# A hybrid Fourier/Hyena block on one core: the long convolution's first transform stage as two 64-row matmuls, and PSUM handed out in pairs of banks

## The chip, the cores and the metric

The kernel runs on 1 core of one Trainium2 chip. The metric is the device time in microseconds (us), the median over several executions. Everything is float32 at the borders; inside, some products use a split of each operand into two halves (`fp32r`), others are plain float32.

## What is computed

One layer of an encoder block over 2048 positions and 1024 channels. Cut to what matters here:

```
p   = rmsnorm(x) @ W_in               -> Fourier group | x1 | x2 | v   (512 columns each)
y_f = rmsnorm(Re(FFT2 of the Fourier group))
z   = v
for n, gate in enumerate((x1, x2)):   # 512 channels
    z = gate * (irfft(rfft(z, 4096) * rfft(k_n)) [:2048] + z * d_n)
y_h = rmsnorm(z)
x   = x + concat(y_f, y_h) @ W_out
x   = x + relu(rmsnorm(x) @ W_fc1)^2 @ W_fc2
out = rmsnorm(x)
```

The change sits in the loop over `n`, the two long convolutions. Each real transform of length 4096 is done as two small DFTs. The first one is a product with a table of 32 input rows, the same for every residue of the position; then comes a rearrangement, and then a second product with one 128x128 table for each of 32 frequencies.

## The kernel before, in words

The program is one Python function that writes out every instruction. A tile framework adds the semaphores and allots buffers; each engine then executes its own instructions strictly in the order in which they were written, save where the program raises the priority of a few lines (none of these are in the part that changes). The stages in order, with the time at which they lie in the profiled run:

- 0 to 413 us: two passes of `project` (lines 319 to 440), 32 + 32 accumulations `pu` of 24 matmuls each, and beside the first of them the filters' hidden layers and a product of weights.
- 413 to 618 us: `fourier` (449) and `filters` (499), which makes the spectra of the eight filters and stores them in DRAM.
- 618 to about 826 us: `hyena` (677), the convolutions.
- from there to the end at 2296 us: `project_out` (901), `fc1` (1116) and `fc2` (1233), long rows of 512-column matmuls.

**The convolutions.** `hyena` works through eight blocks, for n = 0, 1 and four groups of 128 channels (`ct`). The data lies in `zz`, 128 partitions by 16 by 512; a partition holds one of two halves of the positions (`sp`), one of 32 positions and one of two interleaved parts. A block has these steps:

- `first(c)`, lines 712 to 719, for c = 0 to 7: the first DFT for 16 channels. Two matmuls (line 718), one for each half `sp`, with the weights `e1[:, sp, :]` (128x128) and 256 moving columns each, into the left and right half of one PSUM bank `pz1`. The table `e1z` (lines 60 to 65) holds zeros in the 64 rows that belong to the other half, so half of each product is a sum of zeros. Then VectorE turns the bank into `G` (`turned`, lines 444 to 446, a stream transpose of 512 elements per partition).
- `second(q)`, lines 721 to 734, for q = 0 to 7: four matmuls of 128 columns (725) read `G`; ScalarE copies the result into `zs` with its halves exchanged (728, 729), VectorE multiplies it by the spectrum `ks` into `y` (731), GpSimd multiplies `zs` by `ks` (732), and one of the two adds both (733). `ks` is loaded by SyncE's DMA queue (704), with four buffers.
- `inverse(q)`, 736 to 742: four matmuls (741) read `y`; ScalarE copies into `V` (742).
- `turn(c)`, 744 to 747, for c = 0 to 7: VectorE turns `V` into `W`.
- `gate(q)`, 749 to 757, for q = 0 to 3: two matmuls of 64 output rows and 512 columns (754) into the upper and the lower half of the partitions of one bank `pb`; VectorE multiplies by the gate into `zz` (755).

The order is written out by hand (759 to 803). In round i, block i does `second(0)` to `second(7)`. Beside it run the `inverse` of the same block, three steps later (`LAG`), the `turn`s of block i-1, the four `gate`s of block i-2 at q = 1, and the `first`s of block i+1 as `FIRSTS` says: before, two at each of q = 0 and 1, one at each of q = 2, 3, 4 and 5. Block 0 does its eight `first`s ahead of round 0 (768, 769). `first` puts work on TensorE and VectorE alone; it issues no DMA.

**PSUM.** The memory that matmuls write has eight banks of 512 float32 per partition. Every stage takes its banks through one function (168, 169), a ring of eight tiles with one tag:

```
    def pa(nm):
        return ps.tile([P, 512], F32, tag="a", name=nm, bufs=8)
```

A tile's bank comes free when its last reader is done, and a matmul that opens a new tile waits for a free bank; what stands behind it on TensorE waits too. In the profile the names lose their numbers: `pz1` and `pz2` are both `pz`, `pk`, `pk1` and `pk2` are `pk`.

Of the kernel before, what the change touches and what calls it, by code (L numbers as in the profile page):

```python
# [10 lines left out]
F32 = mybir.dt.float32  # L11
# [118 lines left out]
P = 128  # L130
# [6 lines left out]
def hybrid_block(ctx: ExitStack, tc: tile.TileContext, A, out):  # L137
    nc = tc.nc
# [23 lines left out]
    ps = ctx.enter_context(tc.tile_pool(name="ps", bufs=2, space=PSUM))  # L162
    small = ctx.enter_context(tc.tile_pool(name="small", bufs=8))

    def pool(name, side="left"):
        return tc.tile_pool(name=name, bufs=1, side=side, reuse_waits="tile")

    def pa(nm):
        return ps.tile([P, 512], F32, tag="a", name=nm, bufs=8)

    def load(pl, tag, shape, src, bufs=1):
        t = pl.tile(shape, F32, tag=tag, name=tag, bufs=bufs)
# [49 lines left out]
    def transposed(src, nm):  # L222

        for b in (0, 4):
            pt = pa(f"pt_{nm}")
            for k in range(4):
                nc.tensor.transpose(pt[:, 128 * k : 128 * k + 128], src[:, 128 * (b + k) : 128 * (b + k) + 128], ident)
            yield b, pt.rearrange("p (k t) -> p k t", k=4)
# [4 lines left out]
    def fourier_weights(wp):  # L233

        yield
        rd = load(wp, "rd", [P, P], A["rdft"])
        wt = {}
        for k in range(9):
            if k < 8:
                t = load(wp, "wf", [P, 512], A["w_in"][128 * k : 128 * k + 128, 0:512], 2)  # L240
                p = pa("pwt")
                for c in range(4):
                    nc.tensor.transpose(p[:, 128 * c : 128 * c + 128], t[:, 128 * c : 128 * c + 128], ident)
                wt[k] = wp.tile([P, 4, 128], F32, tag="wt", name="wt", bufs=2)
                nc.scalar.copy(wt[k], p.rearrange("p (c d) -> p c d", c=4))
            if k:
                p = pa("pwr")
                for c in range(4):
                    nc.tensor.matmul(p[:, 128 * c : 128 * c + 128], lhsT=wt[k - 1][:, c, :], rhs=rd, start=True, stop=True)
                wr = wp.tile([P, 512], F32, tag="wr", name="wr", bufs=2)  # L250
                nc.scalar.mul(wr, p, gmix[:, k - 1 : k])
                nc.sync.dma_start(wfd[128 * k - 128 : 128 * k, :], wr)
            yield
# [187 lines left out]

    def turned(dst, c, src):

        nc.vector.transpose(dst.rearrange("p c f e -> p c e f")[:, 8 * c : 8 * c + 8], src)


    def fourier(fp, uf, e1f, ffs):
# [3 lines left out]
        for c in range(16):  # L453
            p = pa("pf1")
            nc.tensor.matmul(p, lhsT=e1f, rhs=ufv[:, :, :, 16 * c : 16 * c + 16], start=True, stop=True)
            turned(G, c, p.rearrange("p (x c e) -> p c e x", c=8, e=2))
            yield
# [41 lines left out]
    def filters(ctx, tp, fx, fp, gp, zp, zzs, norms, emb, wo, e1k, f2, dk8, tabs):  # L499
# [10 lines left out]
        class Unit:  # L510
# [76 lines left out]
            def stage1(self, c):  # L587
                if c == 0 and self is units[7]:

                    self.G = fp.tile([P, 64, 32, 2], F32, tag="kh", name="Gk")  # L590
                elif c == 0:
                    self.G = gp.tile([P, 64, 32, 2], F32, tag="Gk", name="Gk")
                p = pa("pk1")
                mm3(p, e1h, e1l, self.k[0][:, c], self.k[1][:, c], True, True)
                turned(self.G, c, p.rearrange("p (l c e) -> p c e l", c=8, e=2))
# [81 lines left out]
    def hyena(hp, wp, rp, zz, e1, b1, f2, a2, work):  # L677
# [3 lines left out]
        def big(nm):  # L681
            return (rp if nm == "W" else wp).tile([P, 64, 32, 2], F32, tag=nm, name=nm, bufs=1 if nm == "W" else 2)

        class Block:
# [27 lines left out]
            def first(self, c):  # L712
                if c == 0:
                    self.G = big("G")
                p = pa("pz1")
                lo = 128 * self.ct + 16 * c
                for sp in range(2):
                    nc.tensor.matmul(p[:, 256 * sp : 256 * sp + 256], lhsT=e1[:, sp, :], rhs=zz[:, :, lo : lo + 16], start=True, stop=True)
                turned(self.G, c, p.rearrange("p (l c e) -> p c e l", c=8, e=2))

            def second(self, q):
                ks = self.ahead.pop(q) if q in self.ahead else self.spectrum(q)
# [36 lines left out]
        LAG = 3  # L759
        TURNS = ((0,), (1,), (2, 3), (4, 5), (6, 7))  # L760
        LAST = ((0,), (1, 2), (3, 4), (5, 6), (7,))
        FIRSTS = ((0, 1), (2, 3), (4,), (5,), (6,), (7,), (), ())
        blocks = [Block(n, ct) for n in range(2) for ct in range(4)]
        for k in range(4):
            blocks[0].ahead[k] = blocks[0].spectrum(k)

            nc.sync.dma_start(a2[:, 8 * k : 8 * k + 8], A["a2"][:, 8 * k : 8 * k + 8])
        for c in range(8):
            blocks[0].first(c)
        for i in range(8):  # L770
            cur, old, older, new = (blocks[j] if 0 <= j < 8 else None for j in (i, i - 1, i - 2, i + 1))
            for q in range(8):
# [28 lines left out]
                if new:  # L801
                    for c in FIRSTS[q]:
                        new.first(c)
# [633 lines left out]
    zz, = zzs  # L1437
    b1 = load(tabs.enter_context(pool("tabs2", "right")), "b1", [P, P], A["b1"])
    with pool("raws") as rp:
        with pool("wts") as wp:  # L1440
            work = Out(wp, zp, zz, gy)
            with pool("hyena") as hp:
                hyena(hp, wp, rp, zz, e1z, b1, f2h[0], f2, work)
            tabs.close()

            raws = rp.tile([P, 32, 128], F32, tag="W", name="W").rearrange("p (n f) c -> p n (f c)", n=4)
            b = {}
            with pool("op") as op:
                first = project_out(op, work, raws, b)
            with pool("fc1") as mp:  # L1450
                begun = fc1(mp, raws, zp, b, *first)
        zstack.close()
# [55 lines left out]
```

## Time and profile before

| | |
|---|---|
| median of three runs | 2302.65 us (2300.39, 2302.65, 2302.73) |
| the profiled execution's own time | 2297.96 us |
| its span, first to last instruction | 2296.2 us |
| granted TensorE clock, mean | 0.993 |
| TensorE matmuls, busy | 2237.3 us, 97% of the span |
| VectorE busy | 1509.3 us, 66% |
| ScalarE busy | 1110.5 us, 48% |
| GpSimd busy | 824.8 us, 36% |
| all first-stage matmuls of the convolutions (line 718) | 256 records, 618.1 to 789.9 us |

A plain float32 matmul leaves two records in the trace, each with its own weight load, so the two matmuls of one `first` are four records of 256 columns. The end of a matmul's record is modelled: records overlap, and TensorE's pace is read from the start of one group to the start of the next. "PEld" is the weight load, which normally lies under the matmul before it. A row of the timeline gives start, length, engine, line, operation, out<-in, the number of records merged, and in brackets the idle time of the engine before it with what ended it. A row of the windows view gives a stretch, its length, and the busy time of each engine in it, then the granted clock, the share of the DMA engines' time and GB/s.

### The profile page before, as it was taken

How to read it: one execution, taken by the hardware profiler on the slowest of the kernel's cores; microseconds unless marked ns; L12 is line 12 of the kernel's file. 1: busy time of each engine (PE TensorE's matmuls, PEld its weight loads, DVE VectorE, ACT ScalarE, POOL GpSimd, SP SyncE). 2: the span in 40 equal slices, each digit the busy share in tenths (PEclk: the TensorE clock that was granted, in tenths of full speed). 3: DMA queues.
4: the chain of work that ended last, by engine and by line, in shares of the span. 5: the costliest groups of instructions: out<-in, count | busy, mean ns of one | idle time of the engine just before them, and what ended most of it. 6: DMA issues, size and time to landing. Idle time of an engine off the chain costs nothing.

```text
span 2296.2 us, 31043 instructions
## 1 busy us (share of the span) xinstructions
PE 2237.3 (97%) x11025; PEld 1853.2 (81%) x11025; DVE 1509.3 (66%) x2258; ACT 1110.5 (48%) x1849; POOL 824.8 (36%) x623
## 2 busy tenths in 40 slices
PE   8999999999899989998999989999999999999998
PEld 6887788799788858887888878888888888888886
DVE  6999776778678774458444465444476666866667
ACT  6555211566366564456555565555543333533333
POOL 3344323677376611146555556555400000000000
PEclk9999999999999999999999999999999999999999
DMA  8545886689987766667444475444489766866631
GB/s 266 181 140 187 329 303 245 226 292 319 324 274 208 216 195 187 178 202 234 158 149 150 150 250 162 152 152 151 142 315 346 245 190 195 299 195 193 192 119 74
DMA packets 298797, 487.31 MB, mean 212 GB/s; under 512 B 17477, under 2 KB 141711, under 8 KB 294417
## 3 DMA queue, kind: packets, MB, share of 16 engines
q1 hardware_dynamic: 292977, 470.91, 62.5%
q10 hardware_dynamic: 5664, 14.41, 1.8%
q8 instruction: 87, 1.43, 0.3%
q14 instruction: 69, 0.57, 0.1%
HBM read 314.64 MB, written 169.05 MB: 211 GB/s over the span
## 4 chain that ended last, share of the span: by engine, by line
PE 78%; DVE 4%; DMA 3%; ACT 2%; issue 1%; POOL 1%; SPq 0%; ACTq 0%; DVEq 0%; POOLq 0%
PE p2u L193 5%; PE p2u L192 5%; PE p2u L194 5%; PE p1u L192 5%; PE p1u L194 5%; PE p1u L193 5%; PE p2v L193 3%; PE p2v L192 3%; PE p2v L194 3%; PE pu L194 2%; PE pu L193 2%; PE pu L192 2%; PE p1v L192 2%; PE p1v L194 2%; PE p1v L193 2%; PE po L192 2%
## 5 line engine op out<-in xcount | busy, mean ns | idle before, releaser
L184 ACT CAST qahm<-ra 128x1024 fp32r<-128x1024 f32 x110 | 115.9, 1053 | 344.5 <-PE p2u L193 172.0
L185 DVE TENSOR_TENSOR qalm<-ra,qahm 128x1024 fp32r<-128x1024 f32 x110 | 134.7, 1225 | 153.8 <-ACT qahm L184 151.8
L1282 POOL TENSOR_TENSOR acc<-acc,gfin 128x512 f32<-128x512 f32 x4 | 5.1, 1276 | 631.9 <-DMA out<-acc 624.7
L192 PE MATMUL pu<-wh,xh 128*128 128x512 f32 x512 | 204.4, 400 | 4.8 <-ACT wh L187 3.6
L193 PE MATMUL pu<-wl,xh 128*128 128x512 f32 x512 | 201.7, 394 | 3.6 <-DVE wl L188 3.5
L194 PE MATMUL pu<-wh,xl 128*128 128x512 f32 x512 | 201.2, 393 | 0.2 <-DVE xl L185 0.2
L193 PE MATMUL p2u<-qblm,qahm 128*128 128x512 f32 x504 | 196.1, 389 | 0.0
L192 PE MATMUL p2u<-qbhm,qahm 128*128 128x512 f32 x504 | 195.8, 389 | 0.0
L194 PE MATMUL p2u<-qbhm,qalm 128*128 128x512 f32 x504 | 195.8, 389 | 0.0
L185 DVE TENSOR_TENSOR qblm<-rb,qbhm 128x1024 fp32r<-128x1024 f32 x110 | 134.1, 1219 | 3.5 <-ACT qbhm L184 3.0
L383 POOL TENSOR_TENSOR acc<-acc,cw 128x512 f32<-128x512 f32 x45 | 59.9, 1331 | 201.6 <-DVE acc L360 200.3
L184 ACT CAST ahm<-s 128x512 fp32r<-128x512 f32 x124 | 76.6, 621 | 100.6 <-PE p1v L193 55.3
L185 POOL TENSOR_TENSOR alm<-W,ahm 128x512 fp32r<-128x512 f32 x63 | 85.5, 1357 | 99.7 <-ACT ahm L184 93.1
L193 PEld LDWEIGHTS pu<-wl,xh 128*128 128x128 f32 x512 | 97.3, 190 | 25.6 <-DVE wl L188 4.9
L184 ACT CAST qbhm<-rb 128x1024 fp32r<-128x1024 f32 x110 | 115.3, 1048 | 5.4 <-DMA rb<-in_w_fc 4.2
L192 PEld LDWEIGHTS pu<-wh,xh 128*128 128x128 f32 x512 | 97.1, 190 | 25.7 <-ACT wh L187 4.0
L194 PEld LDWEIGHTS pu<-wh,xl 128*128 128x128 f32 x512 | 97.2, 190 | 21.3 <-DVE xl L185 1.1
L192 PEld LDWEIGHTS p2u<-qbhm,qahm 128*128 128x128 f32 x504 | 94.6, 188 | 20.2 <-issue 0.3
L193 PEld LDWEIGHTS p2u<-qblm,qahm 128*128 128x128 f32 x504 | 94.6, 188 | 19.6
L194 PEld LDWEIGHTS p2u<-qbhm,qalm 128*128 128x128 f32 x504 | 94.6, 188 | 19.5
L192 PE MATMUL p1u<-bm,ahm 128*128 128x512 f32 x252 | 100.2, 398 | 8.1 <-ACT ku L1144 8.1
L184 ACT CAST ahm<-W 128x512 fp32r<-128x512 f32 x94 | 57.5, 615 | 100.9 <-PE p1u L193 98.8
(397 smaller groups left out, 6429.5 us busy)
## 6 DMA issues: line engine op xcount, KB each, us to landing
W<-in_w_fc SPq DMA_DIRECT2D x66, 512.0 KB
spec<-ks SPq DMA_DIRECT2D x32, 1024.0 KB
ks<-spec SPq DMA_DIRECT2D x64, 512.0 KB
rb<-td SPq DMA_DIRECT2D x64, 512.0 KB
ra<-a1m SPq DMA_DIRECT2D x56, 512.0 KB
ra<-a0m SPq DMA_DIRECT2D x54, 512.0 KB
rb<-in_w_fc SPq DMA_DIRECT2D x46, 512.0 KB
f<-in_w_fc SPq DMA_DIRECT2D x16, 1024.0 KB
```

The lines of the kernel that those rows point to most:

```text
L184: nc.scalar.copy(hi, src)
L185: (eng or nc.vector).tensor_sub(lo, src, hi)
L192: nc.tensor.matmul(o, lhsT=lh, rhs=rh, start=start, stop=False, skip_group_check=more)
L193: nc.tensor.matmul(o, lhsT=lh, rhs=rl, start=False, stop=False, skip_group_check=more)
L194: nc.tensor.matmul(o, lhsT=ll, rhs=rh, start=False, stop=stop, skip_group_check=more)
L383: nc.gpsimd.tensor_add(m1, m1, cw[:, 3, :])
L1282: nc.gpsimd.tensor_mul(acc[i][:, c], acc[i][:, c], gfin[:, c])
```

## The change

`first` now handles 32 channels: four calls for a block in place of eight. Each of its two matmuls takes only the 64 partitions of its half `sp`, of the weights and of the data, streams 512 columns, and writes a bank of its own. The two banks are neighbours, so that one stream transpose of 1024 elements per partition reads both. To have neighbours, PSUM becomes a ring of four tiles of two banks; `pa` hands out the left half of a new pair and at the next call the right half of the same pair. A pair is one tile: it comes free when the last reader of both halves is done. `FIRSTS` now has one `first` at each of q = 0, 1, 3 and 5, and block 0 does four ahead of round 0.

```diff
+    spare = []
+
+    def pair(nm):
+        return ps.tile([P, 1024], F32, tag="a", name=nm, bufs=4)
+
     def pa(nm):
-        return ps.tile([P, 512], F32, tag="a", name=nm, bufs=8)
+        if spare:
+            return spare.pop()
+        t = pair(nm)
+        spare.append(t[:, 512:1024])
+        return t[:, 0:512]
...
-    def turned(dst, c, src):
+    def turned(dst, c, src, n=8):
 
-        nc.vector.transpose(dst.rearrange("p c f e -> p c e f")[:, 8 * c : 8 * c + 8], src)
+        nc.vector.transpose(dst.rearrange("p c f e -> p c e f")[:, n * c : n * c + n], src)
...
             def first(self, c):
                 if c == 0:
                     self.G = big("G")
-                p = pa("pz1")
-                lo = 128 * self.ct + 16 * c
+                p = pair("pz1")
+                lo = 128 * self.ct + 32 * c
                 for sp in range(2):
-                    nc.tensor.matmul(p[:, 256 * sp : 256 * sp + 256], lhsT=e1[:, sp, :], rhs=zz[:, :, lo : lo + 16], start=True, stop=True)
-                turned(self.G, c, p.rearrange("p (l c e) -> p c e l", c=8, e=2))
+
+                    h = slice(64 * sp, 64 * sp + 64)
+                    nc.tensor.matmul(p[:, 512 * sp : 512 * sp + 512], lhsT=e1[h, sp, :], rhs=zz[h, :, lo : lo + 32], start=True, stop=True)
+                turned(self.G, c, p.rearrange("p (l c e) -> p c e l", c=16, e=2), 16)
...
-        FIRSTS = ((0, 1), (2, 3), (4,), (5,), (6,), (7,), (), ())
+        FIRSTS = ((0,), (1,), (), (2,), (), (3,), (), ())
...
-        for c in range(8):
+        for c in range(4):
             blocks[0].first(c)
```

## The prediction

> **What bounds the kernel now.** I read the page first, then the windows round by round of the convolutions, then TensorE's timeline of one round, and last the stretch in which TensorE is not dense.
>
> ```profile
> PE 2237.3 (97%) x11025; PEld 1853.2 (81%) x11025; DVE 1509.3 (66%) x2258; ACT 1110.5 (48%) x1849; POOL 824.8 (36%) x623
> ```
> ```profile
> 648.18:673.19 25.01, 24.66 (x180) 23.10 (x178) 19.85 (x31) 19.94 (x34) 19.22 (x18) 1.00 0.78 234
> 673.19:698.18 24.99, 24.99 (x177) 21.48 (x176) 22.34 (x36) 14.63 (x25) 17.32 (x16) 1.00 0.77 230
> 698.18:723.17 24.99, 24.99 (x177) 21.47 (x176) 20.28 (x33) 14.62 (x25) 16.52 (x15) 1.00 0.71 212
> ...
> 748.16:773.15 24.99, 24.99 (x177) 21.47 (x176) 20.37 (x33) 14.63 (x25) 16.02 (x15) 1.00 0.71 213
> ```
>
> The stretches run from one round's gates to the next round's. A round takes 24.99 us and TensorE is busy for all of it, at a granted clock of 1.00. VectorE is second with 20.3 us, 22.3 in round 2. A busy column alone proves little, because ends of matmuls are modelled, so the starts decide:
>
> ```profile
> 695.47 1.89 PE L718 MATMUL pz<-zz,e1z 128*128 128x256 f32 x8
> 697.20 1.05 PE L725 MATMUL pz<-G,f2h 128*128 128x128 f32 x8
> 698.18 3.66 PE L754 MATMUL pb<-W,b 128*64 128x512 f32 x16
> 701.77 1.16 PE L741 MATMUL pv<-y,f 128*128 128x128 f32 x8
> 702.77 1.89 PE L718 MATMUL pz<-zz,e1z 128*128 128x256 f32 x8
> 704.50 1.06 PE L725 MATMUL pz<-G,f2h 128*128 128x128 f32 x8
> 705.39 1.05 PE L741 MATMUL pv<-y,f 128*128 128x128 f32 x8
> 706.28 1.03 PE L718 MATMUL pz<-zz,e1z 128*128 128x256 f32 x4
> 707.15 1.06 PE L725 MATMUL pz<-G,f2h 128*128 128x128 f32 x8
> ```
>
> No row has an idle bracket, and the steps repeat: second and inverse 0.89 us each, one `first` 0.87, two 1.73. TensorE issues without a hole, so in these rounds a microsecond taken off it is a microsecond off the end, as long as VectorE and the banks keep up. In the chain that ended last,
>
> ```profile
> PE 78%; DVE 4%; DMA 3%; ACT 2%; issue 1%; POOL 1%; SPq 0%; ACTq 0%; DVEq 0%; POOLq 0%
> ```
>
> TensorE has 78%, most of it in the rows behind the convolutions, which start when these end; so what is saved here reaches the end.
>
> **The price of the new first stage.** A round has eight `first`s: two doubles and four singles, 2 x 1.73 + 4 x 0.87 = 6.94 us. What the half-height pair costs no row shows; the nearest thing is the gate, whose two matmuls use half of the array's columns each. For scale, 512 columns in the whole array:
>
> ```profile
> 413.06 1.88 PE L455 MATMUL pf<-uf,e1f 128*128 128x512 f32 x4
> 414.78 1.05 PE L532 MATMUL pk<-wo,emb 128*128 128x128 f32 x8
> ```
>
> Four records in 1.72 us: 0.43 each. The gates' 16 records of 512 columns would then take 6.88 us one after another, but start to next start is 3.59 (698.18 to 701.77). So the two halves of the array really run side by side: 8 slots of 0.43, that is 3.44, and 0.15 more. There is a toll at the borders as well: the second before the gates takes 0.98 instead of 0.89 (697.20 to 698.18), the inverse behind them 1.00 instead of 0.89 (701.77 to 702.77). Together 0.15 + 0.09 + 0.11 = 0.35 for each switch, however many gates stand between.
>
> A new `first` has four records of 512 columns, so two slots, 0.86, and as each stands alone between an inverse and a second, it pays one switch: 0.86 + 0.35 = 1.21. One part of that may be larger here:
>
> ```profile
> L718 PEld LDWEIGHTS pz<-zz,e1z x256: 187/190/192, 618.0 to 789.6; 128*128 128x128 f32 x128
> L754 PEld LDWEIGHTS pb<-W,b x112: 132/133/137, 673.2 to 843.5; 128*64 128x64 f32 x112
> ```
>
> The weight load of a gate has 64 columns and takes 133 ns; mine has 128 columns and takes 190, and the first load of a switch is not hidden. I add 0.04 and take 1.25. Bounds: 1.05 if the toll is mostly a feature of column halves, 2.11 if there is no overlap at all (four slots, 1.72, and 0.39). I take the gate's behaviour because it is the same array, the same data type, the same column count, and only the direction of the cut differs. A round then needs 4 x 1.25 = 5.00 in place of 6.94: 1.94 us less.
>
> **VectorE** turns the same elements with half as many instructions.
>
> ```profile
> L446 DVE STREAM_TRANSPOSE G<-pz 128x512 f32<-128x512 f32 x64 | 43.9, 699 | 15.0 <-PE pz L718 13.4
> L185 DVE TENSOR_TENSOR qalm<-ra,qahm 128x1024 fp32r<-128x1024 f32 x110 | 134.7, 1225 | 153.8 <-ACT qahm L184 151.8 <-issue 1.8
> L185 DVE TENSOR_TENSOR eblm<-W,ebhm 128x512 fp32r<-128x512 f32 x2 | 1.4, 685 | 0.6 <-ACT oyn L932 0.6
> ```
>
> No row has a transpose of 1024 elements. In another operation doubling the elements turns 685 ns into 1225, so 145 ns of each instruction are fixed; the same for the transpose gives 2 x 699 - 145 = 1253 ns, at worst 1398. VectorE saves 0 to 0.6 us a round. A round of 23.05 us on TensorE still holds 20.3 - 0.6 = 19.7 us of VectorE: 85%, so on the average it does not become the bound. But the multiplication `y` now sometimes stands behind a transpose of 1.25 instead of 0.70 us. The chain from a second to its inverse:
>
> ```profile
> L728 ACT ACTIVATE zs<-pz 64x512 f32<-64x512 f32 x64 | 38.1, 595 | 36.3 <-PE pz L725 31.2 <-POOL zs L732 4.4
> L729 ACT COPY zs<-pz 64x512 f32<-64x512 f32 x64 | 37.0, 578 | 0.8
> L732 POOL TENSOR_TENSOR zs<-zs,ks 128x512 f32<-128x512 f32 x64 | 85.1, 1330 | 45.1 <-ACT zs L729 38.6 <-DMA ks<-spec 2.8 <-POOL ks L709 2.3
> L733 POOL TENSOR_TENSOR y<-y,zs 128x512 f32<-128x512 f32 x30 | 38.4, 1281 | 3.6 <-DVE y L731 1.3
> ```
>
> That is 0.89 + 0.60 + 0.58 + 1.33 + 1.28 = 4.7 us. The inverse is written three steps later; with the new places of `first` the shortest such distance, from q = 5, is 0.89 of the step's own inverse, 1.25, two steps of 1.78 and a second, 6.6 us. So 1.9 us are spare for queueing, and a transpose that is 0.55 longer fits.
>
> **Where nothing is gained.** Block 0's eight `first`s and round 0:
>
> ```profile
> 618.14 7.07 PE L718 MATMUL pz<-zz,e1z 128*128 128x256 f32 x32
> 626.02 1.16 PE L725 MATMUL pz<-G,f2h 128*128 128x128 f32 x8 [0.81 <-DVE G L446]
> ```
> ```profile
> 630.91 0.29 ACT L707 COPY ks<-ks 1x128 f32<-1x128 f32 x1 [11.48 <-DMA ks<-spec]
> ```
> ```profile
> 618.00:626.00 8.00, 7.21 (x35) 6.03 (x33) 5.74 (x8) 1.07 (x2) 0.00 (x0) 1.00 1.01 360
> 626.00:650.00 24.00, 22.70 (x160) 20.98 (x160) 10.88 (x17) 11.26 (x21) 13.92 (x15) 1.00 1.05 354
> ```
>
> The first stage would end some 2 us sooner (four transposes of 1.25 us behind the first pair end near 624.2), but the first spectrum lands at 630.9 whatever TensorE does: the DMA engines are full (share 1.01 and 1.05, 354 GB/s) until 650. What TensorE saves in round 0 it waits away. Gain 0.
>
> **The banks.** `pa` and `pair` keep all eight banks in use, but a bank comes back only with its neighbour. The single takers mostly come in even numbers that belong together (two outputs of one projection, four `p2u`, four `p2m`), so pairs hold what is born and dies together. In `fc2` the three sets of four are six pairs of which four are ever alive, two sets at a time; in `fc1` a step opens three banks, u and v live into the next step, and at most three pairs are held. An even number of single banks is taken ahead of each of these stages, so the sets start on a pair's left half. I put all that at nothing, covered by the fourth pair; without the cover TensorE would wait where a pair is opened, below 1 us each. Two places are tight. The first is the start of the Fourier stage:
>
> ```profile
> 417.68 1.05 PE L532 MATMUL pk<-wo,emb 128*128 128x128 f32 x8
> ...
> 420.51 1.98 PE L455 MATMUL pf<-uf,e1f 128*128 128x512 f32 x4 [1.77 <-DVE kt L536]
> ```
>
> TensorE waits until VectorE has emptied a bank. With pairs it runs out one tile sooner, and the way back needs two releases: 0 to 1.05 us, one tile; I take 0.5. The second is round 1, where VectorE is behind after the late spectra:
>
> ```profile
> 646.54 1.16 PE L725 MATMUL pz<-G,f2h 128*128 128x128 f32 x8 [0.40 <-DVE G L446]
> ```
> ```profile
> 651.36 0.68 DVE L731 TENSOR_TENSOR y<-pz,ks 128x512 f32<-128x512 f32 x1
> ...
> 653.21 0.68 DVE L731 TENSOR_TENSOR y<-pz,ks 128x512 f32<-128x512 f32 x1
> ```
>
> The second of 646.54 has its bank read only at 653.21, 6.7 us later, because spectra and adds of round 0 come first. A new round opens 14 pairs (20 banks of second, inverse and gate, and four pairs of `first`) in 23 us, 1.65 us apart; four pairs bear a life of 4 x 1.65 = 6.6 us. With lives of 6.7 the `first` of round 1 must wait for a pair, and behind it on TensorE's queue stand the next second and inverse. I put round 1 at no gain at all (between 0 and 1.94), and round 2, where VectorE has 22.3 us of work, at 0.5 less. From round 3 on
>
> ```profile
> 706.81 0.69 DVE L731 TENSOR_TENSOR y<-pz,ks 128x512 f32<-128x512 f32 x1 [1.39 <-ACT zs L729]
> ```
>
> a life is 3.0 us (second at 704.50, bank read out at 707.50) and nothing waits.
>
> **The sum:** rounds 2 to 6, 5 x 1.94 = 9.7; less 0.5 in round 2, less 0.5 in the Fourier stage: 8.7 us. From the profiled execution's 2297.96 that is 2289.3; the median of the runs shown lies 4.7 higher (2302.65), so 2294.0.
>
> **Rivals.**
> *Passes in order.* A float32 matmul is two records on the same rows; if the second half's first record may not pass the first half's second, only the middle two of four overlap: three slots, 1.29, and the toll of 0.39 make 1.68 against 1.735 for the two old ones. Rounds 2 to 6 gain 20 x 0.055 = 1.1, and the two losses of 0.5 take it back: 2302.5, no change. For it: nothing shows half rows. Against it: in such an order the gates' 16 records would need nine slots, 3.87 us, and they take 3.59. The Trainium skill, "TensorE: Matmul & The Clock Gate", section "Part 3: Packing small matmuls — row/col tiling", calls matmuls strictly first-in first-out; the gates' rows agree with that only if the records of the two halves already alternate in the queue.
>
> *Half overlap.* The two streams may slow each other, as each now writes all 128 partitions of PSUM where a gate's writes 64. Halfway between two slots and four is again three slots, 2302.5. The same section of the same page measured 3.07 times the speed for four tiles of a quarter of the rows, 77% of ideal; an estimate from it is 0.86 / 0.77 = 1.12 for the two slots, 1.51 a `first` and 2299.2 in all.
>
> *VectorE and the banks eat it.* If each of rounds 2 to 6 loses a further 1 us because `y` stands behind a long transpose or a pair is late, 8.7 - 5 = 3.7 is left: 2299.0. For it: in round 2 VectorE would have 22.3 - 0.6 = 21.7 us of work in 23.05, 94%. Against it: lives of 3 us later on.
>
> *No overlap, slower.* The halves run one after another; each `first` takes 2.11 where two took 1.735. On the dense rounds 1 to 6 that is 24 x 0.375 = 9.0 us, and 0.5 in the Fourier stage: 2312.2. It decides from 1.735 a `first` upward, and the change then simply doesn't do what it says. For it: no row shows two row halves together. Against it: the gates.
>
> **How the numbers follow.** Forecast 0.72; passes in order 0.08; half overlap 0.05; VectorE and banks 0.07; no overlap 0.08. What can be told from no change here is 0.2%, 4.6 us. The forecast's own range comes from the bounds of a `first` (1.05 to 1.4 over 20 of them: 4 us better, 3 worse) and of the bank waits (2 us either way): 2288 to 2299. Widened to the three middle rivals it is 2288 to 2303, and only the slower one lies outside. Faster by more than 0.2%: the forecast, 0.72; within 0.2%: the three middle ones, 0.20; slower: 0.08.
>
> **What would show it.** In a dense round: 4 records of 512 columns at line 718, from their start to the next second's 1.0 to 1.2 us, with two records starting together; a round of about 23.05 us; transposes of 1024 elements near 1.25 us. Right in the banks' part: waits of TensorE on VectorE between 648 and 660, and none from round 3 on. Wrong would be records of line 718 one after another 0.43 apart (no overlap), a second that waits for `G` in every round (VectorE), or idle brackets on TensorE in the feed-forward stages (the pairs hold banks there).

## The result, and the profile after

| | median | against before on the same chip |
|---|---|---|
| before | 2302.69 us (2300.39 to 2305.20) | |
| after | 2435.94 us (2434.81 to 2436.60) | 1.0578, 95% interval 1.0560 to 1.0596: slower, 133 us |

The profiled execution after took 2434.81 us, its span is 2433.0. The page's first lines and its chain of the work that ended last:

```profile
PE 2293.1 (94%) x10897; PEld 1819.9 (75%) x10897; DVE 1513.1 (62%) x2226; ACT 1116.1 (46%) x1849; POOL 815.7 (34%) x623
...
PE 66%; DVE 8%; DMA 5%; ACT 5%; issue 4%; POOL 2%; SPq 0%; DVEq 0%; ACTq 0%; POOLq 0%
```

TensorE has 66% of the chain instead of 78%: more of the time to the end now goes to other engines and to handing work from one to the next. And the loss isn't in the stage that was rewritten. TensorE's timeline gives the starts of the stages, the first Fourier matmul, the first `first` and the first `fc1` matmul, before at 408.4, 618.14 and

```profile
1041.70 0.48 PE L192 MATMUL p1u<-zf,eahm 128*128 128x512 f32 x1
```

and after:

```profile
448.12 1.02 PE L465 MATMUL pf<-uf,e1f 128*128 128x512 f32 x2
...
680.99 1.12 PE L730 MATMUL pz<-zz,e1z 64*128 64x512 f32 x2
...
1137.16 0.77 PE L202 MATMUL p1u<-zf,eahm 128*128 128x512 f32 x1
```

Ahead of the convolutions 62.9 us are lost, 40 of them in `project`, which has no `first` in it (the windows view has TensorE idle there for 43.6 us in place of 16.1; the other 12 us are longer busy time, which was not traced to a cause); in the convolutions and `project_out` 32.6 (456.2 in place of 423.6); from `fc1` on 41.3 (1295.8 in place of 1254.5).

What the first stage itself costs stands in TensorE's timeline of a dense round:

```profile
841.22 1.16 PE L737 MATMUL pv<-G,f2h 128*128 128x128 f32 x8
842.31 1.13 PE L730 MATMUL pz<-zz,e1z 64*128 64x512 f32 x4
843.37 1.16 PE L737 MATMUL pv<-G,f2h 128*128 128x128 f32 x8
844.37 1.94 PE L753 MATMUL pv<-y,f 128*128 128x128 f32 x16
...
846.52 1.16 PE L737 MATMUL pv<-G,f2h 128*128 128x128 f32 x8 [0.21 <-ACT V L754]
```

Four records of 64 rows take 1.06 us to the next start, where two old firsts took 1.73; the half-height matmuls do run side by side. But the window of that round has

```profile
829.54:857.24 27.70, 26.23 (x162) 17.48 (x161) 20.90 (x29) 14.32 (x25) 16.02 (x14) 1.00 0.66 191
```

27.70 us in place of 24.99. The names tell what happened. A second (line 737, it reads `G`) now writes `pv`, the name of an inverse's tile: it has the right half of the pair that an inverse opened. Two inverses stand at 844.37 one behind the other, and the second behind them waits for "ACT V": for ScalarE to copy out the left half, which holds the inverse. In the convolutions this wait comes to 9.2 us in 22 times, 2.1 us at the longest (total, times, longest):

```profile
PE pv L737 <- ACT V L754: 9.2, 22, 2.1
```

The same in `project`, ScalarE and TensorE:

```profile
212.64 0.59 ACT L355 COPY xc<-pt_x 128x512 f32<-128x512 f32 x1
...
213.28 0.50 PE L202 MATMUL pt_x<-wh,xh 128*128 128x512 f32 x1 [0.72 <-ACT xc L355]
```

A product that needs nothing from that `xc` waits until the transposes in the left half are copied out, and only then writes the right half. TensorE's waits over the projections, in total (who waited for whom, us, times, the longest):

```profile
PE pu L204 <- DVE xl L195: 15.3, 8, 4.1
...
PE pt_x L202 <- ACT xc L355: 3.9, 4, 2.2
PE pt_x L237 <- ACT xc L355: 3.7, 5, 1.5
```

Before, the same wait for `xl` came to 0.2 us, and none for `xc` stands in the answer.

### The profile page after: what moved, and what is told of

Read it like the earlier page. It is cut to its first block, busy times and chain, and to the rows that moved or that the text cites. A ratio compares the mean times of both kernels' runs of the same rounds, so it can differ in the third digit from the quotient of the medians.

```text
span 2433.0 us, 30776 instructions
## 1 busy us (share of the span) xinstructions
PE 2293.1 (94%) x10897; PEld 1819.9 (75%) x10897; DVE 1513.1 (62%) x2226; ACT 1116.1 (46%) x1849; POOL 815.7 (34%) x623
## 4 chain that ended last, share of the span: by engine, by line
PE 66%; DVE 8%; DMA 5%; ACT 5%; issue 4%; POOL 2%; SPq 0%; DVEq 0%; ACTq 0%; POOLq 0%
PE p2u L202 5%; PE p2u L203 4%; PE p2u L204 4%; PE p1v L202 4%; PE p1v L203 3%; PE p1v L204 3%; PE p1u L202 3%; PE p1u L204 3%; PE p1u L203 3%; PE p2v L202 2%; PE p2v L203 2%; PE p2v L204 2%; PE po L202 2%; PE po L204 2%; PE po L203 2%
## 5 line engine op out<-in xcount | busy, mean ns | idle before, releaser
L204 PE MATMUL pu<-wh,xl 128*128 128x512 f32 x392 | 156.0, 400 | 15.3 <-DVE xl L195 15.3
L202 PE MATMUL pu<-wh,xh 128*128 128x512 f32 x392 | 157.0, 403 | 10.3 <-DVE m L370 3.5
L203 PE MATMUL pu<-wl,xh 128*128 128x512 f32 x392 | 155.3, 397 | 0.5 <-DVE wl L198 0.5
L1323 DVE TENSOR_TENSOR acc<-acc,p2u 128x512 f32<-128x512 f32 x128 | 87.0, 683 | 31.9 <-PE p2u L204 31.5
L744 POOL TENSOR_TENSOR zs<-zs,ks 128x512 f32<-128x512 f32 x64 | 84.5, 1325 | 62.7 <-ACT zs L741 60.1
L202 PE MATMUL p1v<-bm,ahm 128*128 128x512 f32 x252 | 100.0, 397 | 2.9 <-DVE c L1092 2.8
L203 PE MATMUL p1v<-bm,ahm 128*128 128x512 f32 x252 | 98.5, 391 | 3.4 <-DVE bm L195 3.4
```

What stands on the lines that cost most here:

```text
L202: nc.tensor.matmul(o, lhsT=lh, rhs=rh, start=start, stop=False, skip_group_check=more)
L203: nc.tensor.matmul(o, lhsT=lh, rhs=rl, start=False, stop=False, skip_group_check=more)
L204: nc.tensor.matmul(o, lhsT=ll, rhs=rh, start=False, stop=stop, skip_group_check=more)
L744: nc.gpsimd.tensor_mul(zs, zs, ks[:, 1])
L1323: nc.vector.tensor_add(t, t, held[bank, j])
```

## The experiments

Theory A: the pairs couple two banks that have nothing to do with each other. A1, by a false order (a write of one half waits for the reader of the other); A2, by late release (four pairs that come back only when both halves are read are too few banks). Theory B: the new first stage costs the time.

**1. The pairs alone.** The kernel before with `pa` and `pair` of the change, the old first stage:

```
...
     def pa(nm):
-        return ps.tile([P, 512], F32, tag="a", name=nm, bufs=8)
+        if spare:
+            return spare.pop()
+        t = pair(nm)
+        spare.append(t[:, 512:1024])
+        return t[:, 0:512]
```

> The kernel before with one half of the change alone: PSUM as four pairs of banks, single banks taken as halves of a pair. The first stage stays as it was, 256 columns per matmul on all 128 rows, into a single bank. Theory A, the pairs couple the two halves (either way, by order or by late release): nearly the whole loss of 133 us is here, 2425 to 2455 us, and the Fourier stage starts near 448 us as after the change, not near 408. Theory B, the new first stage itself costs the time: no change, 2300 to 2306.

Measured: 2446.97 us against 2301.69, ratio 1.0637 (1.0619 to 1.0655), 145 us slower; the Fourier stage starts at 454.2. The whole loss, and more, is the pairs'; with the new first stage on top the loss is some 12 us smaller. B has fallen.

**2. The first stage alone.** `pair_mode` closes the PSUM pool and opens it again: eight single banks outside, six singles and one pair in rounds 0 to 6.

```
+    def pair_mode(on):
+        banks.close()
+        held[:] = [banks.enter_context(tc.tile_pool(name="ps", bufs=2, space=PSUM, reuse_waits="tile")), 6 if on else 8]
...
+    def pair(nm):
+        return held[0].tile([P, 1024], F32, tag="b", name=nm, bufs=1)
...
+    def pa(nm):
+        return held[0].tile([P, 512], F32, tag="a", name=nm, bufs=held[1])
```

> The kernel after with the other half alone: the half-height first stage into a pair, but eight single banks everywhere outside the convolutions, and in the convolutions' rounds 0 to 6 six single banks and one pair that only the first stage takes. Nothing else shares a tile. Theory A: the loss is gone and the gain of the first stage shows. In the trace after, four half-height matmuls take 1.06 us from start to next start where two old first stages took 1.73, so about 0.6 us x 4 = 2.4 a round less a toll at the borders; rounds 1 to 6 give 9 to 14 us: 2289 to 2294. Theory B: the loss stays in the convolutions, above 2340.

Measured: 2323.23 us, ratio 1.0098 (1.0083 to 1.0113). The big loss is gone, as A has it, but no gain shows: 21.5 us slower than before, nearly all of it between the first `first` and `fc1`, and three of the four rounds after the first gates take 26.9 us. That misses the expected 2289 to 2294 by some 30 us, so there is a second cause; it is taken up below.

**3. The false order off.** The kernel after, with all its pairs; at the end of the program every two instructions that touch different halves of one pair, and share no other tensor, are declared free of each other:

```
...
+def unlink(nc, tc, psum):
...
+                if not sx & sy and not rx & ry:
+                    tc.declare_no_dep(x, y, reason="different banks")
```

> The kernel after, with all its pairs, but the framework is told that an instruction that touches only the left half of a pair and one that touches only the right half need not wait for each other (different banks). A pair still comes back only when both halves have been read. It parts two forms of theory A. A1, false order: the write of one half waits for the reader of the other half; with that order gone nearly the whole loss is gone, 2290 to 2305, the sum of the prediction with its small losses for late pairs. A2, late release: four pairs are too few when both halves must be read first; then the time stays above 2400. Between them: each has its share.

Measured: 2313.88 us against 2301.69, ratio 1.0057 (1.0042 to 1.0072). That is 9 us above the range expected for A1, but of 133 us 121 are gone with the order and nothing else; the Fourier stage starts at 407.0 again, TensorE's waits in the projections hold no `xc` and 0.4 us for `xl`, and the chain of the page reads

```profile
PE 76%; DVE 4%; DMA 3%; ACT 2%; POOL 2%; issue 2%; SPq 0%; POOLq 0%; ACTq 0%; DVEq 0%
```

From the first `fc1` matmul to the end it takes 1254.6 us, as before the change (1254.5). This is A1. 12 us stay.

**4. Six banks.** The kernel before with the pool of experiment 2 and the old first stage, so that two banks lie idle in rounds 0 to 6.

> The kernel before, old first stage, eight single banks outside the convolutions, but only six single banks in their rounds 0 to 6 (two banks lie idle there). It prices the number of banks by itself, for reading the kernel with six singles and a pair. Banks enough: 2300 to 2306. A round opens 28 banks in 25 us, 0.89 apart, so six banks bear a life of 5.4 us; lives of 6.7 us in rounds 0 and 1 could cost 1 to 4 us there: up to 2307. If the number of banks were the cause of the loss (A2), more: above 2315.

Measured: 2305.93 us, ratio 1.0021 (1.0011 to 1.0031). The dense rounds are 24.99 us as before: six banks are enough. 2.2 us are lost between the gates of round 7 and the next gates (27.81 in place of 25.62), next to the place where the pool is exchanged. The convolutions start at 621.8 in place of 618.1; experiment 6, which leaves the banks as they were, has 622.0, so the later start is no sign of what six banks cost.

**The second cause.** Experiment 2's timelines of ScalarE, VectorE and TensorE at the end of a round:

```profile
779.47 0.63 ACT L756 COPY V<-pv 128x512 f32<-128x512 f32 x1
782.61 0.29 ACT L719 COPY ks<-ks 1x128 f32<-1x128 f32 x1 [2.51 <-DMA ks<-spec]
782.93 0.59 ACT L742 ACTIVATE zs<-pz 64x512 f32<-64x512 f32 x1
```
```profile
784.15 0.69 DVE L745 TENSOR_TENSOR y<-pz,ks 128x512 f32<-128x512 f32 x1 [2.33 <-ACT zs L743]
784.75 0.70 DVE L458 STREAM_TRANSPOSE W<-V 128x512 f32<-128x512 f32 x1
785.57 0.69 DVE L747 TENSOR_TENSOR y<-y,zs 128x512 f32<-128x512 f32 x1
786.17 1.25 DVE L458 STREAM_TRANSPOSE G<-pz 128x1024 f32<-128x1024 f32 x1
```
```profile
780.75 1.13 PE L732 MATMUL pz<-zz,e1z 64*128 64x512 f32 x4
...
784.59 1.05 PE L755 MATMUL pv<-y,f 128*128 128x128 f32 x8
787.57 1.47 PE L739 MATMUL pz<-G,f2h 128*128 128x128 f32 x8 [1.92 <-DVE G L458]
788.84 1.91 PE L755 MATMUL pv<-y,f 128*128 128x128 f32 x8
790.68 1.57 PE L732 MATMUL pz<-zz,e1z 64*128 64x512 f32 x4
```

ScalarE copies one row of the next block's first spectrum, and stands 2.51 us before a DMA that has not landed. The `zs` of a second that ended at 779.8 runs at 782.93; VectorE stands for it; behind that in VectorE's queue is the transpose of the last first, whose matmuls (780.75) were through at about 781.9; and TensorE's next block cannot begin without `G`. In the kernel before the same copy came behind one more `zs` and found its data there (ScalarE was idle for 0.02 us ahead of it):

```profile
740.10 0.62 ACT L742 COPY V<-pv 128x512 f32<-128x512 f32 x1
740.74 0.30 ACT L707 COPY ks<-ks 1x128 f32<-1x128 f32 x1
741.24 0.59 ACT L728 ACTIVATE zs<-pz 64x512 f32<-64x512 f32 x1 [0.20 <-PE pz L725]
```

Here the description of the kernel ahead of the prediction has to be put right: the framework does not keep to the written order. It moves instructions ahead (by what rule, no run shows), and it does so with this copy: written at the start of step 7, behind the `zs` of step 6, it runs ahead of the `zs` of steps 5, 6 and 7 in experiment 2, of 6 and 7 in the kernel before.

**5. The copy behind.** Experiment 2, with the copy (and GpSimd's two fills) written into the block's `second(0)` and an order edge behind the last `zs`:

```
...
+                if q == 0:
+                    fix = nc.scalar.copy(ks[64:65, 0, 0, :], ks[64:65, 1, 0, :])
+                    if last_zs:
+                        tc.add_manual_dep(fix.ins, last_zs[0], mybir.DependencyInfo(mybir.DependencyClass.NoSync, mybir.DependencyReason.SCHED_ONLY), reason="behind the last zs")
...
```

> Eight single banks outside, six singles and a pair in the convolutions, half-height first stage (as in the kernel with six singles and a pair), and one thing more: ScalarE's copy of one row of the next block's first spectrum (and GpSimd's two fills behind it) is ordered behind the last zs of the block at hand; it read 2.5 us of waiting for that spectrum's DMA in each round, 0.02 before the change. Theory C, this wait is what ate the first stage's gain: zs, y and the transposes of the last first stand behind it, and a second waits 2 us for G. A dense round falls from 26.9 to about 23.1 us (19.07 without a hole up to the place, and 2 seconds, an inverse and a first, 3.93), the whole to 2292 to 2303. Rival D, six single banks are too few for the faster round: the round stays above 25 us and the whole above 2310.

Measured: 2311.27 us against 2300.06, ratio 1.0048 (1.0031 to 1.0065). The rounds after the first gates took 26.96, 25.32, 26.86 and 26.86 us in experiment 2 and take 27.37, 24.04, 23.51 and 23.78 here, and some 10 us of the 21.5 are gone: C is right about three of the rounds (not quite at 23.1), and the whole misses the expected 2292 to 2303 by 8 us. D isn't what holds it: rounds 0 and 1 do, 63.9 us from the first `first` to the first gate in place of 55.1, where the four firsts of block 0 wait for one another's transposes (1.35 us three times) and a second for `G` (4.41 us). One pair is too few there.

**6. The control.** The kernel before with the copy behind.

> The control: the kernel before with only that copy ordered behind the last zs. Its wait was 0.02 us in the dense rounds of the kernel before, so theory C expects no change, 2299 to 2305. If the order of the copy is worth something by itself, it shows here: below 2297.

Measured: 2301.71 us, ratio 1.0001 (0.9992 to 1.0011). As C has it, the copy costs nothing in the kernel before.

**7. Full height.** Experiment 5 with all 128 rows in the first stage's matmuls:

```
-                    nc.tensor.matmul(p[:, 512 * sp : 512 * sp + 512], lhsT=e1[h, sp, :], rhs=zz[h, :, lo : lo + 32], start=True, stop=True)
+                    nc.tensor.matmul(p[:, 512 * sp : 512 * sp + 512], lhsT=e1[:, sp, :], rhs=zz[:, :, lo : lo + 32], start=True, stop=True)
```

> As the kernel with the copy behind, but each first stage's two matmuls use all 128 rows (half of the weights are zero) and 512 columns, into the same pair and with the same transposes: what the pair and the wider transpose give without the half-height overlap. If the overlap is the gain, a first takes four slots of 0.43, 1.72 from start to next start in place of 1.06, and a round 4 x 0.46 = 1.8 us more (no toll at the borders): 24.9 us, and the whole 9 to 12 us above the half-height kernel. If the gain came from fewer transposes or places, the two are within 3 us.

```profile
755.55 1.88 PE L729 MATMUL pz<-zz,e1z 128*128 128x512 f32 x4
757.27 1.06 PE L742 MATMUL pz<-G,f2h 128*128 128x128 f32 x8
758.17 1.05 PE L758 MATMUL pv<-y,f 128*128 128x128 f32 x8
```

A first takes 1.72 us and no toll, a dense round 24.95, as in the kernel before. Measured: 2317.57 us, ratio 1.0076 (1.0059 to 1.0093), 6.3 above the half-height kernel instead of 9 to 12, since that one's dense rounds take 23.5 to 24.0, not 23.1. So the gain is the overlap, not the fewer transposes or the places.

**8. Both causes off.** The kernel after, the false order off, the copy behind.

> The kernel after with all its pairs, the false order between halves off, and the copy ordered behind the last zs. Theory: false order and the waiting copy together are the whole difference from the prediction (2294.0): 2290 to 2303, a dense round near 23.1 us. If late release of pairs costs something of its own, this kernel is slower than the one with six singles, a pair and the same order of the copy, by that amount.

Measured: 2304.44 us against 2300.06, ratio 1.0015 (1.0005 to 1.0025); dense rounds of 23.6 to 23.7 us. It is faster than experiment 5, so four pairs for everybody bear the convolutions better than six singles and one pair; it lies 1.4 us above the expected 2290 to 2303. A second still waits for `G` at the start of a block: 1.93 us in round 2, 0.26 to 0.37 in a dense round, 2.89 in round 7.

**9. The firsts earlier.** Experiment 8 with

```
-        FIRSTS = ((0,), (1,), (), (2,), (), (3,), (), ())
+        FIRSTS = ((0,), (1,), (2,), (3,), (), (), (), ())
```

> As the kernel with the false order off and the copy behind, and the four first stages of a round at steps 0, 1, 2 and 3 in place of 0, 1, 3 and 5. In that kernel the second that opens a block still waits for G, the transpose of the last first: 1.9 us in round 1 to 2, 0.3 in each dense round, 2.9 in round 6 to 7. Theory E, the wide transpose behind y in VectorE's queue is what is late: with the last first two steps earlier these waits go, about 6 us: 2296 to 2301, a dense round 23.3 us. Rival F, VectorE as a whole is behind (21.9 us of work in 23.7): the wait moves to y or zs, and the time stays within 2 us of 2304.

Measured: 2298.68 us against 2301.49, ratio 0.9989 (0.9980 to 0.9997): 2.8 us faster than the kernel before, 0.7 to 4.6 by the interval. The waits for `G` after round 1 are gone, E is right. A dense round in the windows and in TensorE's timeline:

```profile
750.70:774.06 23.36, 23.33 (x161) 16.97 (x160) 21.69 (x29) 14.63 (x25) 16.11 (x15) 1.00 0.75 226
```
```profile
757.46 1.05 PE L759 MATMUL pv<-y,f 128*128 128x128 f32 x8
758.45 1.13 PE L730 MATMUL pz<-zz,e1z 64*128 64x512 f32 x4
759.50 1.16 PE L743 MATMUL pv<-G,f2h 128*128 128x128 f32 x8
760.50 1.05 PE L759 MATMUL pv<-y,f 128*128 128x128 f32 x8
```

Inverse 0.99 (0.89 between equals), first 1.05, second 1.00 (0.89): a first costs 1.05 + 0.10 + 0.11 = 1.26 us with its borders. Block 0 of the same run has four firsts in a row:

```profile
623.84 3.70 PE L730 MATMUL pz<-zz,e1z 64*128 64x512 f32 x16
```

Its records start in pairs, the first two pairs 0.53 us apart, all later ones 0.42: two pairs, 0.85 us, for each first that stands behind another. So the 1.26 of a lone first is full overlap and a price for the change at each end, as the prediction has it.

**10. Late release by itself.** Experiment 1 with the false order off.

> The kernel before with the pairs alone (old first stage), which took 2447 us, and the false order between the halves of a pair off. What is left is that a pair comes back only when both halves have been read. Theory A1 (false order is the whole of the pairs' loss): 2299 to 2306. Late release costs something of its own: 2306 to 2320, and then the kernels with pairs owe that much to it.

Measured: 2305.56 us against 2301.49, ratio 1.0017 (1.0009 to 1.0026). Of the 145 us of the pairs 141 are false order; what is left, late release with it, is 4 (2 to 6 by the interval). The dense rounds are 24.99 us, so these 4 lie outside of them. The convolutions begin at 623.4, and at 623.8, 623.9 and 623.8 in the other kernels with pairs and no false order, against 618.1 to 622.0 in seven of the eight with single banks there and 627.9 in the eighth (the full-height one); that the pairs hold the start back fits, but the spread is as large as the effect.

**11. Four singles and two pairs.** No shared pair and nothing declared away; experiment 5 with four singles and two pairs in rounds 0 to 6, and the firsts early:

```
...
-        held[:] = [banks.enter_context(tc.tile_pool(name="ps", bufs=2, space=PSUM, reuse_waits="tile")), 6 if on else 8]
+        held[:] = [banks.enter_context(tc.tile_pool(name="ps", bufs=2, space=PSUM, reuse_waits="tile")), 4 if on else 8]
...
-        return held[0].tile([P, 1024], F32, tag="b", name=nm, bufs=1)
+        return held[0].tile([P, 1024], F32, tag="b", name=nm, bufs=2)
...
```

> No shared pair at all and no order declared away: eight single banks outside the convolutions, in their rounds 0 to 6 four single banks and two pairs that only the first stage takes, the copy ordered behind the last zs, the firsts at steps 0 to 3. Against six singles and one pair (2311) the second pair lets a block's firsts follow one another while the last is being transposed. If a single pair was what held rounds 0 and 1 back (64 us from the first first stage to the first gate, 55 before): 2296 to 2303. If four single banks are too few for second, inverse and gate (20 banks in 23 us, lives up to 4.6 us): above 2308.

Measured: 2303.88 us, ratio 1.0008 (1.0000 to 1.0017), just above the expected range: not faster than before. Rounds 0 and 1 are better (57.5 us to the first gate, not 63.9), and the dense rounds are 23.9 us, each with one wait for `y`. Whether four singles or the one exchange of the pool takes the last 2 us was not parted.

**12. Pairs in the convolutions alone.** Experiment 9, with eight single banks outside the rounds 0 to 6.

> Eight single banks outside the convolutions; in their rounds 0 to 6 four pairs, of which first stages take whole ones and everything else halves, with the false order off; the copy behind; the firsts at steps 0 to 3. The pairs alone with the false order off took 2305.6 against 2301.5 and began the convolutions near 623.5 us, as did every kernel with pairs throughout, against 618 to 622 with single banks: late release costs 2 to 4 us ahead of the convolutions. With singles there that comes back, and the 5 us that the kernel with early firsts gained from the first first stage to the first fc1 matmul (418.7 against 423.6) stays: 2294 to 2298, faster than both. If the start near 623.5 is not owed to the pairs, it stays at 2298 to 2301.

Measured: 2300.25 us against 2301.00, ratio 0.9995 (0.9985 to 1.0005): no difference, and a miss. The convolutions begin at 620.1 as hoped and the dense rounds are 23.36, but between the gates of rounds 6 and 7 lie 24.59 us where experiment 9 has 22.55. All the kernels that exchange the pool at round 7 lose 2 to 4 us there or a round later (experiments 2, 4, 5, 7 and 11 too); that the exchange does it is likely, and was not tried by itself.

## Why the prediction was wrong, point by point

- **The price of the first stage**: right. 1.25 predicted, 1.26 measured, and the terms agree too (1.05 from the first's start to the next, 0.10 and 0.11 at the borders; predicted 1.05, 0.09 and 0.11), with records that start in pairs; the rivals with no overlap, half overlap and passes in order are out. The transposes of 1024 elements:

```profile
L456 DVE STREAM_TRANSPOSE G<-pz x32: 1208/1239/1251, 689.1 to 877.7; 128x1024 f32<-128x1024 f32 x32
```

  1.239 us, predicted 1.253.
- **"I put all that at nothing"**: this step failed, and with it the result. The prediction asked of the pairs only how long they are held, and found the cover for that nearly sufficient: late release, with whatever else is left without the order, costs some 4 us (experiment 10), where it said 0.5 and 0.5 in round 2. It did not ask whether the two halves of one tile are ordered against each other. In this framework they are, although they are different banks: a pair handed to two takers turns "write one while the other is read" into "one after the other". That is 121 of the 133 us (experiment 3), 141 of 145 without the new first stage (experiment 10). Small programs of a few such instructions (built, not run) have three such waits: a write of the right half after a read of the left, a read of the left after a write of the right, and a read of one half after another engine's read of the other. With the declarations of experiment 3 all three are gone, and a new pair still waits for the readers of both halves of the old one. The prediction's own sign of error, idle brackets on TensorE in the feed-forward stages, is there; its reason for them, that pairs hold banks, isn't the one.
- **"1.9 us are spare for queueing, and a transpose that is 0.55 longer fits"**: this failed on a small scale. The chain from second to inverse was counted, but not the copy of the next spectrum in ScalarE's queue, whose place the framework chose anew: 0.02 us of waiting became 2.5 a round, worth 8 to 10 us (experiments 3 to 8, 2 to 5). Nor was the distance from the last first to the next block's first second: moving the last first two steps ahead, and the one before it one step, took another 7 us off (8 to 9).
- **Rounds 0 and 1 gain nothing**: right; 55.1 us from the first `first` to the first gate before, 56.0 in experiment 9.
- **A dense round of 23.05 us**: 23.36 when nothing stands in the way. From the first gate to the sixth, five rounds, 123.2 us become 116.8 in experiment 9: 6.4 gained where 9.2 were forecast (9.7 less the 0.5 in round 2), and 2.8 in the whole. Where the other 3.6 go is not shown; in the profiled runs the convolutions begin 5.7 us later than before, but other kernels vary there as much (experiment 10). With both causes off and the firsts moved, a third of the predicted 8.7 is left.

## What to carry to other kernels

Before sharing one tile among unrelated takers, ask what the framework tracks: how long a buffer is held is only one price, and an order between its parts was many times that here (141 us and some 4). When a stage gets shorter, look at what other engines do in their own queues beside it, such as a copy that waits for a DMA; its wait was hidden by the old length. And try the two halves of a change by themselves first: the half that looked like bookkeeping was the whole result.

## What the runs showed of the hardware

A short hole in TensorE's work can cost more than its length. In experiment 2, TensorE stands about 2 us before 787.57, and the windows before and behind show the granted clock:

```profile
767.50:785.40 17.90, 17.90 (x128) 13.32 (x124) 12.94 (x19) 8.89 (x17) 10.45 (x10) 1.00 0.68 208
787.40:793.20 5.80, 5.63 (x28) 4.39 (x28) 5.59 (x8) 2.78 (x5) 2.84 (x3) 0.71 0.68 198
```

In the records the distance of the 128-column matmuls is 0.11 us until 788.20, then 0.21, and from about 791.65 on 0.11 again: some 3.4 us at half speed, beginning 0.6 us after the hole was over. But it is not the length of the hole alone that decides. From its first gates on, experiment 2 has five such holes, each of 1.92 to 2.01 us before a second that waits for `G`. Behind four of them a stretch runs at half speed; behind this one all is at full speed:

```profile
735.45 1.13 PE L739 MATMUL pz<-G,f2h 128*128 128x128 f32 x8 [1.99 <-DVE G L458]
736.42 1.05 PE L755 MATMUL pv<-y,f 128*128 128x128 f32 x8
```

That is why one of the rounds takes 25.32 us where the two behind it take 26.86: the same hole, and 1.5 us for the clock. A hole of 2.42 us in experiment 9 (before 810.07) has no slow stretch behind it either. What decides it is not shown. The Trainium skill, "TensorE: Matmul & The Clock Gate", section "Part 1: The HAM clock gate (the "warmup" mystery)", has the clock halved by windows of about 3.4 us, which the length of the slow stretch agrees with; it puts the fall behind an idle window of that length, and here holes of 2 us were enough, four times in five.

Two float32 matmuls in the two row halves of the array, 512 columns each into neighbouring banks, start 7 ns apart. A group of four records that stands alone takes 1.06 us where the full height takes 1.72, 1.62 times the speed, or 1.37 with the borders counted (1.26). In a row of such groups, as in block 0 of experiment 9, each takes 0.85 us: twice the speed.
